# Feed-forward projections: 512-column and 256-column products in runs of eight, or in turn

## The chip, the core and the metric

The kernel runs on one core of a Trainium2 chip. TensorE multiplies matrices and writes to PSUM, VectorE and ScalarE compute on tiles, GpSimd does a few small things, and DMA queues, driven by SyncE, move data from and to device memory. The metric is the device time of one execution, in microseconds, as the median of several runs. All times below are microseconds unless marked ns.

## The reference

A model of two layers on 256 tokens of width 1024, in float32. Each layer is a feed-forward block, a mixer (a gated delta rule with a state-space branch in the first layer, sparse attention in the second) and another feed-forward block; each is followed by a layer norm over the block's output and the scaled input. The change lies in the feed-forward blocks, four of them in all:

```python
D_MODEL, SEQ, D_FF = 1024, 256, 2816

def swiglu(x, w_in, w_out):
    gate, up = jnp.split(x @ w_in, 2, axis=-1)
    return (jax.nn.silu(gate) * up) @ w_out

for layer in range(DEPTH):
    h = layer_norm(DEEPNORM_ALPHA * h + 0.5 * swiglu(h, ffn_w_in[layer, 0], ffn_w_out[layer, 0]), ...)
    ...
    h = layer_norm(DEEPNORM_ALPHA * h + 0.5 * swiglu(h, ffn_w_in[layer, 1], ffn_w_out[layer, 1]), ...)
```

## The kernel before

**Numbers in two parts.** TensorE reads its operands in a reduced float32 format. To keep the accuracy, each operand is split into a high part (the value rounded to that format) and a low part (the rest). A product is then high times high, plus low times high, plus high times low. For weights, `split` does this: a copy to `whi` (ScalarE, or VectorE where the planner finds that better) and a subtraction into `wlo` (always VectorE). The activations `x` are kept as one tile that holds, for each of 8 blocks of 128 input channels, the 256 tokens' high parts and next to them their 256 low parts.

**The feed-forward block** (`ffn`). For each block of 128 of the 2816 hidden channels, `proj_two` computes the gate and then, in a second call, the up projection: 8 blocks of input channels are summed into one PSUM bank `ps` of 512 columns. The weights stand still in the array and the activations move through it. With the high weights `w[0]`, all 512 columns of `x[2]` go through (high and low activations: two of the three products at once). With the low weights `w[1]`, only the 256 high columns go through, and add to the bank's first 256 columns. A projection is thus 8 matmuls of 512 columns and 8 of 256. Then `add_two` adds the two halves of the bank (a copy by ScalarE, an addition by VectorE), ScalarE applies silu to the gate, VectorE multiplies, and the result `g` is split. Between two such pairs of projections the output products of an earlier block run (`out_mm`, four accumulators `acc`, 12 matmuls of 512 columns). The first one or two steps of a block (256 hidden channels each) take another path, token by token (`proj_tok`), and are not touched. That leaves 20 hidden blocks in the first feed-forward block and 18 in each of the other three.

**What sets the order.** All stages record their operations in a plan; `Plan.order` then simulates the engines with a table of costs, picks at each moment the operation that can start first (by priority where several can), hands out buffers, and may choose between engines where an operation has an alternative. The program is written out in that order, and each engine runs its own list in order. In TensorE's list the matmuls of one projection mostly stand in the order in which `proj_two` records them; here and there the planner puts a transpose between them. Buffers: 4 raw weight tiles of 2048 columns, 36 tiles of 1024 columns for everything else, of which the split weights may hold 12 to 24; 2 banks `ps`, 2 `mp` and 4 `acc`.

**Names in the profile.** All instructions carry line 529, where the plan is written out, so tiles tell them apart. `ps<-x,whi` with 512 columns and `ps<-x,wlo` with 256 columns are the two kinds of matmul of `proj_two`, and `acc<-whi,g` and `acc<-wlo,g` the output products; `PEld` are the loads of weights into the array.

Of the kernel before, what the change touches and what calls it, by code (L numbers as in the profile page):

```python
# [21 lines left out]
KD = D // P  # L22
# [530 lines left out]
class K:  # L553
# [174 lines left out]
    def proj_two(self, x, w):  # L728


        ps = self.bank("ps")
        mm = self.nc.tensor.matmul
        for k in range(KD):
            mm(ps, w[0][:, k, :], x[2][:, k].rearrange("p h b t -> p (h b t)"), start=k == 0, stop=False)
        for k in range(KD):
            mm(ps[:, :T], w[1][:, k, :], self.xk(x, k)[0], start=False, stop=k == KD - 1)
        return ps

# [1267 lines left out]
```

## Time and profile before

| | |
|---|---|
| time, median of 3 runs | 1116.87 (1116.46 to 1117.02) |
| the profiled execution's own time | 1116.44 |
| its span, first to last instruction | 1114.7 |
| matmuls | 6528 |
| matmuls of 512 columns in `proj_two` | 1184 |
| VectorE busy | 878.9 (79%) |
| ScalarE busy | 532.2 (48%) |

A row of the timeline reads: start, time from the first start to the last end, engine, line, operation, tile written and tiles read, shape of the standing operand, shape of the result, count. Neighbours of one kind are merged into one row. Matmuls are pipelined: the next one starts before the one before it has ended, so a row's length says less than the distance of two starts. A row of the chain of waits reads: start, length, engine and tile, count. A row of the groups by shape ends with: busy time, mean ns of one, idle time before them.

### The profile page before, as it was taken

To read this page: it belongs to the slowest core of one execution; us is meant where nothing else is said; L and a number is where in the kernel's file an instruction comes from. 1 tells how busy PE (TensorE), PEld (TensorE's weight loads), DVE (VectorE), ACT (ScalarE), POOL (GpSimd) and SP (SyncE) were. 2 spreads that over 40 slices of the span, in tenths; PEclk is the share of its full clock that TensorE was granted. 3 is DMA by queue.
4 is the path that set the end of the run, shared out by engine and by line. 5 is a ranking of instruction groups with operands and counts; after the bars stand their busy time and mean duration, and the time that the engine had idled before them with its cause. 6 is when DMAs were issued, how large, how long until landed. Compare 5 with 4: busy or idle time off the path is not lost.

```text
span 1114.7 us, 16484 instructions
## 1 busy us (share of the span) xinstructions
PE 1103.0 (99%) x6528; PEld 941.0 (84%) x6528; DVE 878.9 (79%) x1484; ACT 532.2 (48%) x972; POOL 33.8 (3%) x67
## 2 busy tenths in 40 slices
PE   9999999999999999999999999999999999999997
PEld 7888888899999788888888888888878778888886
DVE  8967767878979989777767967876888899677755
ACT  6644333478638656433333633433444766433320
POOL 1000000001000210000000000000000000000000
PEclk9999999999999999999999999999999999999999
DMA  9966563642633385755563755555445128655511
GB/s 332 347 197 213 186 225 113 227 139 76 221 121 133 120 275 186 249 203 177 189 223 115 259 196 193 189 188 160 151 157 184 45 93 281 224 189 201 177 39 38
DMA packets 151672, 201.56 MB, mean 181 GB/s; under 512 B 9565, under 2 KB 127786, under 8 KB 151594
## 3 DMA queue, kind: packets, MB, share of 16 engines
q1 hardware_dynamic: 151594, 200.50, 53.9%
q8 instruction: 51, 0.84, 0.3%
q14 instruction: 27, 0.22, 0.1%
HBM read 197.18 MB, written 1.07 MB: 178 GB/s over the span
## 4 chain that ended last, share of the span: by engine, by line
PE 93%; DVE 4%; DMA 1%; ACT 1%; issue 0%; POOL 0%; SPq 0%; DVEq 0%; POOLq 0%
PE ps L529 57%; PE acc L529 31%; PE mp L529 5%; DVE arena L529 1%; DVE wlo L529 1%; DMA G<-cum 1%; ACT P L529 1%; DVE cv L529 0%; DMA raw<-in_ffn_w_in_dram 0%; ACT G L529 0%; DVE o L529 0%; DVE qs L529 0%; DVE y L529 0%; POOL arena L529 0%; DVE G L529 0%
## 5 line engine op out<-in xcount | busy, mean ns | idle before, releaser
L529 DVE TENSOR_TENSOR wlo<-raw,whi 128x1024 fp32r<-128x1024 f32 (+1 forms) x348 | 415.0, 1214 | 9.5 <-ACT whi L529 6.6
L529 PE MATMUL ps<-x,whi 128*128 128x512 f32 (+1 forms) x1600 | 375.3, 365 | 0.6 <-ACT ktok L529 0.4
L529 PEld LDWEIGHTS ps<-x,whi 128*128 128x128 f32 x1600 | 282.8, 189 | 46.9 <-issue 2.1
L529 ACT ACTIVATE whi<-raw 128x1024 fp32r<-128x1024 f32 (+1 forms) x260 | 262.0, 1050 | 11.5 <-DMA raw<-in_ffn_w_in_dram 9.9
L529 PE MATMUL acc<-whi,g 128*128 128x512 f32 x704 | 230.6, 391 | 0.0
L529 ACT ACTIVATE sg<-ps 128x256 f32<-128x256 f32 x162 | 62.2, 384 | 350.0 <-PE ps L529 349.9
L529 PE MATMUL ps<-x,wlo 128*128 128x256 f32 x1392 | 224.9, 283 | 0.0
L529 PEld LDWEIGHTS ps<-x,wlo 128*128 128x128 f32 x1392 | 201.2, 190 | 11.6
L529 DVE TENSOR_TENSOR sg<-ps,sg 128x256 f32<-128x256 f32 x162 | 68.7, 424 | 161.1 <-ACT sg L529 160.8
L529 PEld LDWEIGHTS acc<-whi,g 128*128 128x128 f32 x704 | 132.5, 188 | 25.9
L529 PE MATMUL acc<-wlo,g 128*128 128x512 f32 x352 | 138.1, 392 | 0.0
L529 PE MATMUL ps<-whi,x 128*128 128x512 f32 (+1 forms) x480 | 129.4, 385 | 0.5 <-DVE whi L529 0.2
L529 PEld LDWEIGHTS ps<-whi,x 128*128 128x128 f32 x480 | 85.9, 189 | 17.7 <-issue 1.6
L529 PEld LDWEIGHTS acc<-wlo,g 128*128 128x128 f32 x352 | 66.4, 189 | 10.9
L529 PE MATMUL ps<-wlo,x 128*128 128x512 f32 (+1 forms) x240 | 67.9, 381 | 0.5 <-DVE wlo L529 0.5
L529 PE MATMUL acc<-whi,x 128*128 128x512 f32 x192 | 64.1, 403 | 0.1
L529 DVE CAST whi<-raw 128x1024 fp32r<-128x1024 f32 (+2 forms) x88 | 59.7, 680 | 1.8 <-PE acc L529 1.3
L529 PEld LDWEIGHTS ps<-wlo,x 128*128 128x128 f32 x240 | 43.2, 188 | 8.1 <-DVE wlo L529 1.2
L529 ACT ACTIVATE sg<-sg 128x256 f32<-128x256 f32 x74 | 31.0, 419 | 33.9 <-DVE sg L529 33.8
L529 DVE SCALAR_TENSOR_TENSOR cv<-cv,arena 128x255 f32<-128x255 f32 (+2 forms) x84 | 39.7, 477 | 5.7 <-ACT cv L529 5.1
L529 PEld LDWEIGHTS acc<-whi,x 128*128 128x128 f32 x192 | 35.6, 188 | 7.5 <-issue 0.5
L529 PE MATMUL acc<-wlo,x 128*128 128x512 f32 x96 | 37.7, 396 | 0.0
(247 smaller groups left out, 950.0 us busy)
## 6 DMA issues: line engine op xcount, KB each, us to landing
raw<-in_ffn_w_in_dram SPq DMA_DIRECT2D x74, 1024.0 KB, 5.1
raw<-in_ffn_w_out_dram SPq DMA_DIRECT2D x44, 1024.0 KB, 5.0
raw<-in_hyb_w_in_dram SPq DMA_DIRECT2D x20, 1024.0 KB, 5.1
raw<-in_ffn_w_in_dram SPq DMA_DIRECT2D x24, 512.0 KB, 5.0
raw<-in_hyb_w_out_dram SPq DMA_DIRECT2D x8, 1024.0 KB, 4.9
raw<-in_nsa_w_in_dram SPq DMA_DIRECT2D x5, 1024.0 KB, 5.2
raw<-in_nsa_w_out_dram SPq DMA_DIRECT2D x4, 1024.0 KB, 5.0
w<-in_nsa_cmp_w_dram SPq DMA_DIRECT2D x8, 512.0 KB, 9.0
```

What stands on the lines that cost most here:

```text
L529: r = getattr(getattr(nc, eng), fn)(*[res(a) for a in args], **{k: res(a) for k, a in kw.items()})
```

## The change

One loop over the 8 blocks of input channels takes the place of two. For each block it issues the matmul with high weights and then the one with low weights; before, eight with high weights came first and then eight with low weights. The sums are the same, added in another order.

```diff
         mm = self.nc.tensor.matmul
         for k in range(KD):
             mm(ps, w[0][:, k, :], x[2][:, k].rearrange("p h b t -> p (h b t)"), start=k == 0, stop=False)
-        for k in range(KD):
             mm(ps[:, :T], w[1][:, k, :], self.xk(x, k)[0], start=False, stop=k == KD - 1)
         return ps
```

TensorE's list at the first two projections of the program, in the first feed-forward block, before (`ps_288` and `ps_328` are the gate's and the up projection's banks, `mp` takes transposes, `acc_359` is the first accumulator of the output products):

```order
L529 MATMUL mp_283<-ident_130,sg_242 128x128 x2
L529 MATMUL ps_288<-x_164,whi_246 128x512 x5
L529 MATMUL mp_302<-ident_130,sg_286 128x128 x2
L529 MATMUL ps_288<-x_164,whi_246 128x512 x3
L529 MATMUL ps_288<-x_164,wlo_255 128x256 x8
L529 MATMUL ps_328<-x_164,whi_267 128x512 x8
L529 MATMUL ps_328<-x_164,wlo_280 128x256 x8
L529 MATMUL acc_359<-whi_297,g_291 128x512
```

The same place after the change, around the second pair of transposes:

```order
L529 MATMUL ps_288<-x_164,wlo_255 128x256
L529 MATMUL ps_288<-x_164,whi_246 128x512
L529 MATMUL mp_304<-ident_130,sg_286 128x128 x2
L529 MATMUL ps_288<-x_164,wlo_255 128x256
L529 MATMUL ps_288<-x_164,whi_246 128x512
```

Three matmuls of 512 columns and three of 256 stand ahead of the second row (the first row is the last of them), in turn, so the low weights `wlo_255` are read from the projection's second matmul on, where they were read from its ninth on. The pair of transposes that stood behind five matmuls of 512 columns now stands behind four of 512 and three of 256.

At the end of the second projection, where the rows before (above) go from eight matmuls on `wlo_280` to `acc_359`, TensorE's list now reads:

```order
L529 MATMUL ps_328<-x_164,wlo_280 128x256
L529 MATMUL ps_328<-x_164,whi_267 128x512
L529 MATMUL ps_328<-x_164,wlo_280 128x256
L529 MATMUL acc_359<-whi_298,g_291 128x512
L529 MATMUL acc_359<-wlo_325,g_291 128x512
```

One matmul of 256 columns stands before the output products, where eight stood. Away from the projections the planner's lists hardly differ: four pairs of transposes stand at another place inside a projection, two copies to `whi` move from ScalarE to VectorE, and in the last block a few operations of ScalarE and VectorE change places by one. The DMAs are the same, in the same order.

## The prediction

> **What bounds the kernel now.** I read the page first (busy time, granted clock, shares of the chain), then the groups by shape, then the chain in order of time, and last the timeline of TensorE in single stretches.
>
> ```profile
> span 1114.7 us, 16484 instructions
> PE 1103.0 (99%) x6528; PEld 941.0 (84%) x6528; DVE 878.9 (79%) x1484; ACT 532.2 (48%) x972; POOL 33.8 (3%) x67
> PEclk9999999999999999999999999999999999999999
> PE 93%; DVE 4%; DMA 1%; ACT 1%; issue 0%; POOL 0%; SPq 0%; DVEq 0%; POOLq 0%
> ```
>
> TensorE is busy for 99% of the span, its clock is granted in full in every slice, and 93% of the chain that ended last is its own. A busy row can overlap its neighbours, so what counts is not the length of a row but the step from the start of one matmul to the start of the next. That step is the whole question here, because the change alters nothing but the order of matmuls.
>
> ```profile
> L529 PE MATMUL ps<-x,whi 128*128 128x512 f32 x1184 | 294.8, 391 | 0.0
> L529 PE MATMUL ps<-x,wlo 128*128 128x256 f32 x1392 | 224.9, 283 | 0.0
> ```
>
> A **long** matmul has 512 columns (high weights), a **short** one 256 (low weights). The 1184 long ones belong to proj_two alone: 8 each, so 148 projections, which the feed-forward blocks make in 74 pairs (gate and up). As many shorts go with them (the other 208 are another stage's).
>
> **The steps now.** The chain in order of time shows one pair of projections as a piece of 32 matmuls on ps, and the output products between pairs as a piece on acc.
>
> ```profile
> 37.65 5.56 PE ps L529 x32
> ...
> 162.25 5.56 PE ps L529 x32
> ...
> 569.49 2.75 PE acc L529 x12
> ...
> 599.99 8.87 PE acc L529 x39
> ```
>
> Both acc pieces are longs that follow a run of shorts. 39 less 12 is 27 more longs in 8.87 - 2.75 = 6.12 us: a settled long steps by **0.2267 us**. Twelve of those make 2.720, and the piece takes 2.75: some 0.03 us is lost once at its head, after the shorts. From 37.65 to 162.25 lie 15 whole periods, 8.307 us each, of 16 + 12 = 28 longs and 16 shorts.
>
> ```profile
> 563.76 1.98 PE L529 MATMUL ps<-x,whi 128*128 128x512 f32 x8
> 565.58 1.11 PE L529 MATMUL ps<-x,wlo 128*128 128x256 f32 x8
> 566.53 2.00 PE L529 MATMUL ps<-x,whi 128*128 128x512 f32 x8
> 568.37 1.12 PE L529 MATMUL ps<-x,wlo 128*128 128x256 f32 x8
> 569.32 0.40 PE L529 MATMUL acc<-whi,g 128*128 128x512 f32 x1
> ```
>
> Here is one pair. The longs of the gate, which follow longs, take 565.58 - 563.76 = 1.82 us; those of the up projection, which follow shorts, take 1.84; eight shorts take 0.95, so 0.119 each, and I use **0.120**. With 0.2267 and 0.120 the period would be 28 x 0.2267 + 16 x 0.120 = 8.267; it is 8.307. The 0.040 left over is the **recovery**: after each of the two short runs of a period the next few longs are together about 0.020 us late. Runs of eight pay for it twice in a period.
>
> **What the change does to the steps.** It adds no instruction and takes none away; 16 shorts and 16 longs of a pair still run, now one by one in turn. The traces hold no stretch of regular alternation, so its step has to be bounded. The nearest rows are in the attention stage, where single short mask products stand among longs.
>
> ```profile
> 858.16 0.28 PE L529 MATMUL ps<-fixed 128*128 128x256 f32 x1
> 858.27 0.40 PE L529 MATMUL ps<-whi,x 128*128 128x512 f32 x1
> 858.50 0.40 PE L529 MATMUL ps<-wlo,x 128*128 128x512 f32 x1
> 858.74 0.39 PE L529 MATMUL ps<-whi,x 128*128 128x512 f32 x1
> 858.97 0.63 PE L529 MATMUL acc<-kd,qs 128*128 128x512 f32 x2
> 859.43 0.28 PE L529 MATMUL acc<-fixed 128*128 128x256 f32 x1
> ...
> 861.84 0.28 PE L529 MATMUL ps<-fixed 128*128 128x256 f32 x1
> 861.95 0.28 PE L529 MATMUL acc<-fixed 128*128 128x256 f32 x1
> 862.07 0.63 PE L529 MATMUL ps<-kd,qs 128*128 128x512 f32 x2
> 862.54 0.28 PE L529 MATMUL ps<-fixed 128*128 128x256 f32 x1
> 862.65 0.62 PE L529 MATMUL acc<-kd,qs 128*128 128x512 f32 x2
> 863.11 0.28 PE L529 MATMUL acc<-fixed 128*128 128x256 f32 x1
> ```
>
> First stretch: one short, then five longs, 859.43 - 858.16 = 1.27 us. The short itself steps by 0.11, less than 0.120, but the five longs after it take 859.43 - 858.27 = 1.16, that is 0.232 each. So a lone short with room to recover costs 1.27 - 5 x 0.2267 = 0.137: one short starts as full a recovery as a run of eight does. Second stretch, the densest mixture in the trace: three shorts and four longs, with no room to recover between, in 863.11 - 861.84 = 1.27 us, and 1.27 - 4 x 0.2267 = 0.363, so 0.121 for each short. There the recovery is cut off before it costs much.
>
> Regular alternation has one long between shorts, nearer to the second stretch than to the first. I take **0.120 + 0.2267 = 0.3467 us** for a short and a long together, and one recovery where the pair ends and the longs of acc begin.
>
> **The sum.** Before, a period has 0.040 of recovery; after, 0.020. That is 0.020 x 74 pairs = 1.5 us less. The profiled execution took 1116.44 us (1114.7 of span and 1.7 around it); 1116.44 - 1.5 = 1114.9. The three runs have their median 0.43 above the profiled execution, at 1116.87, so I predict 1116.87 - 1.5 = **1115.4 us**. For the unknown step both ends are kept: a pair of matmuls may take 0.340 (short at half a settled long, long settled) or 0.363 (0.2267 and the lone short's 0.137).
>
> **What else moves, at nothing.** A projection ends with the same short matmul as before, so ScalarE and VectorE get its bank at the same time. The low weights are needed earlier: after one long instead of eight, so 7 x 0.2267 = 1.6 us sooner. That could be a new wait, above all at the start of the program, where weights have just landed. In the order they are written in, the first projection's low weights are VectorE's row at 16.69, the second's the one at 19.89:
>
> ```profile
> 16.69 1.22 DVE L529 TENSOR_TENSOR wlo<-raw,whi 128x1024 fp32r<-128x1024 f32 x1
> ...
> 19.89 1.22 DVE L529 TENSOR_TENSOR wlo<-raw,whi 128x1024 fp32r<-128x1024 f32 x1
> ```
>
> ```profile
> 20.52 1.41 PE L529 MATMUL ps<-x,whi 128*128 128x512 f32 x5
> ...
> 23.64 2.00 PE L529 MATMUL ps<-x,whi 128*128 128x512 f32 x8
> ```
>
> They are ready at 17.91 and 21.11. In the changed order the first short of these projections is due one long after their start, at 20.75 and 23.87: 2.8 us of room in either. Later ones have more, since the writes run further and further ahead:
>
> ```profile
> L529 DVE TENSOR_TENSOR wlo<-raw,whi x348: 735/1219/1228, 8.0 to 1072.9; 128x1024 fp32r<-128x1024 f32 x171, 128x840 fp32r<-128x840 f32 x2, 128x560 fp32r<-128x560 f32 x1
> L529 PE MATMUL acc<-wlo,g x352: 389/389/481, 26.7 to 1106.6; 128*128 128x512 f32 x176
> ```
>
> The last low weights begin to be written at 1072.9, and the last product that reads such weights starts at 1106.6, over 30 us later. The high weights' buffers come free later, since the last long now stands next to last: by the seven shorts that stood behind it, 7 x 0.120 = 0.8 us. The writer that waits for a buffer is that far ahead of TensorE, and this room hides 0.8; without it each of the 148 projections could lose up to 0.8. Where two transposes stand inside a projection they stay after about as much matmul time: five longs before, 5 x 0.2267 = 1.13, against four longs and three shorts now, 1.27, so what they wait for is no later than they. Two high-weight copies go from ScalarE to VectorE, both off the path (48% and 79% busy). I count all of this as nothing.
>
> **The rivals.**
>
> Rival 1, **the shorts get faster**. A short that follows a long steps by 0.11 in both stretches above, not by 0.120; only the following shorts of a run are at 0.120. In alternation every short follows a long. If the weight load is what holds a run of shorts at 0.120, a long before each short takes that away, and if the longs stay settled the pair is 0.2267 + 0.1133 = 0.340. Sixteen make 5.440, with 2.75 of acc 8.190 against 8.307: 0.117 x 74 = 8.6 us less, 1108.2. For it: the last two longs of the second stretch take 863.11 - 862.65 = 0.46, 0.23 each. Against it: where the short took 0.11 in the first stretch, the next two longs took 0.23 and 0.24, so the gain was given back at once.
>
> ```profile
> L529 PEld LDWEIGHTS ps<-x,wlo 128*128 128x128 f32 x1392 | 201.2, 190 | 11.6
> ```
>
> A load's row lasts 190 ns, more than a short's step, so loads overlap matmuls and the row can't say whether it is the limit. The Trainium skill (TensorE: Matmul & The Clock Gate, LDWEIGHTS (loading the stationary operand)) gives a load as its number of columns over 1.2 ns, an estimate of 107 ns for 128 columns. By that rule the load fits under a step of 0.113, nothing would hold a short at 0.120 once the load starts in time, and this rival's time would come true; the 0.119 of a run of shorts in this trace is longer than the rule gives.
>
> Rival 2, **the recovery never ends**. In runs the longs settle after a few steps and stay at 0.2267 until the next shorts; in alternation each long comes right after a short and none may ever settle. Then every long costs the 0.232 of the first stretch, and the short after an unsettled long has no lead and steps by 0.120: 0.352 for both. Sixteen make 5.632, with 2.75 8.382: 0.075 x 74 = 5.6 us more, 1122.4. This one ends on the other side; it decides from (8.307 - 2.75) / 16 = 0.3473 for both on, where the period gets longer than before. For it: the first two longs after every short run are late. Against: the second stretch.
>
> Rival 3, **a full recovery for each short**, 0.363 for both: 16 x 0.363 + 2.75 = 8.558, 18.6 us more, 1135.5. The second stretch speaks against it, since three shorts there would have cost 0.05 more than they did.
>
> That the change doesn't do what it says can be left out: the order of TensorE's matmuls shows the alternation in all 148 projections.
>
> **How the numbers follow.** My forecast (0.345 to 0.349 for both) has 0.40, rival 1 in full or in part 0.30, rival 2 in full or in part 0.24, rival 3 0.04, and 0.02 are left for a wait on weights or buffers. A change of 0.2%, 2.2 us, is about what a measurement can tell from none; 2.2 / 74 = 0.030 in a period, so it begins at 0.3454 for both below and at 0.3492 above. The forecast's band touches the lower edge, so faster is 0.36, same 0.36, slower 0.28. Cases of both signs hold most of the chance: the forecast's own range is 1113 to 1118. The range for 8 in 10 takes in rivals 1 and 2 in full, 1108.0 to 1123.0, and leaves out rival 3.
>
> **What the changed profile will show.** The chain's piece on ps of 32 matmuls, now 5.56 us, decides: 5.55 by the forecast, 5.44 by rival 1, 5.63 by rival 2, 5.81 by rival 3. The piece on acc should stay at 2.75. TensorE should wait for no low weights near 20 us. I would be wrong if the step of a long depended on something that only alternation has, such as the two column counts writing the same bank in turn, which no row of this trace shows.

## The result, and the profile after

The changed kernel takes 1122.2 us in the median of five runs, against 1116.84 before (five runs): ratio 1.0053, interval 1.0039 to 1.0067. It is slower by 5.4 us, where 1.5 us less was forecast; the time lies within the stated range, near rival 2's 1122.4.

The page after (span and instructions, busy time of the engines, granted clock, shares of the chain that ended last):

```profile
span 1119.8 us, 16483 instructions
PE 1108.6 (99%) x6528; PEld 939.6 (84%) x6528; DVE 880.2 (79%) x1486; ACT 529.8 (47%) x970; POOL 33.8 (3%) x67
PEclk9999999999999999999999999999999999999999
PE 93%; DVE 4%; ACT 1%; DMA 1%; issue 0%; POOL 0%; SPq 0%; DVEq 0%; POOLq 0%
```

The limit is the same: as many matmuls, TensorE 99% busy, clock granted, 93% of the chain. The span is 5.1 us longer, and TensorE's busy time 5.6. TensorE's list of waits holds none above 1.1 us in either kernel, and those that differ are of 0.5 us or less. The time did not go into a wait but into the matmuls' own steps. The chain in order of time shows where:

```profile
457.04 8.17 PE acc L529 x36
...
565.85 5.64 PE ps L529 x32
571.49 2.75 PE acc L529 x12
574.23 5.64 PE ps L529 x32
...
602.32 8.87 PE acc L529 x39
```

The piece of 32 matmuls, a pair of projections, went from 5.56 to 5.64 us; the piece on acc stayed at 2.75. 0.08 x 74 pairs = 5.9 us, a little more than the measured 5.1 of span. One feed-forward block, from the acc piece at its one end to that at the other, shows the same. Its rows in the chain of the kernel before:

```profile
456.06 8.19 PE acc L529 x36
...
599.99 8.87 PE acc L529 x39
```

That is 143.93 us from one start to the other, against 602.32 - 457.04 = 145.28 after: 1.35 more for the block's 18 pairs, 0.075 each.

Inside the piece the timeline after reads (start, length, tiles, shape):

```profile
565.68 0.39 PE L529 MATMUL ps<-x,whi 128*128 128x512 f32 x1
565.91 0.28 PE L529 MATMUL ps<-x,wlo 128*128 128x256 f32 x1
566.02 0.40 PE L529 MATMUL ps<-x,whi 128*128 128x512 f32 x1
566.26 0.28 PE L529 MATMUL ps<-x,wlo 128*128 128x256 f32 x1
566.38 0.40 PE L529 MATMUL ps<-x,whi 128*128 128x512 f32 x1
566.62 0.28 PE L529 MATMUL ps<-x,wlo 128*128 128x256 f32 x1
566.74 0.40 PE L529 MATMUL ps<-x,whi 128*128 128x512 f32 x1
566.97 0.28 PE L529 MATMUL ps<-x,wlo 128*128 128x256 f32 x1
...
569.09 0.28 PE L529 MATMUL ps<-x,wlo 128*128 128x256 f32 x1
```

The first long, which follows the output products, steps by 0.23, and the first short by 0.11. From then on every long is late: 566.02 to 566.26, 566.38 to 566.62, 566.74 to 566.97, 0.23 to 0.24 each against a settled 0.2267. From 565.91 to 569.09 stand nine shorts and nine longs in 3.18 us, **0.3533 us for a short and a long together** where 0.3467 was forecast.

To the nanosecond the trace's starts show a rhythm that repeats every three pairs of matmuls. The table gives, for each step inside a pair of projections and the first matmuls on acc behind it, how much longer it is in ns than a settled long (L, 226.7) or a short within a run (S, 120); it is the mean over the 70 of 74 pairs that no transpose interrupts, rounded; they agree to a nanosecond.

```
before  L0 x8 | S-7 S-1 S0 x6 | L+7 L+9 L+2 L+6 L+4 L0 L0 L0 | S-7 S-1 S0 x6 | L+7 L+9 L+2 L+6 L+4 L0 ...
after   L0 | S-7 L+6 S-3 L+14 S0 L+9 | S-7 L+6 S-3 L+14 S0 L+9 | ... | S-7 | L+6 L+9 L+2 L+6 L+4 L0 ...
```

Before, the sum of a run of shorts and the recovery behind it is -8 + 28 = 20 ns, twice in a period, as the prediction has it. After, the three pairs of a rhythm add up to -7 + 6 - 3 + 14 + 9 = 19 ns (20 unrounded), over and over: every three shorts cost what a run of eight cost before. Five such rhythms and the recovery behind the last short make 120 ns in a period, where two recoveries made 40. In the changed kernel the longs never settle, until the output products give them room.

The low weights came in time. VectorE's first rows, then TensorE's first shorts of the first two projections:

```profile
16.43 1.22 DVE L529 TENSOR_TENSOR wlo<-raw,whi 128x1024 fp32r<-128x1024 f32 x1
...
19.64 1.22 DVE L529 TENSOR_TENSOR wlo<-raw,whi 128x1024 fp32r<-128x1024 f32 x1
```

```profile
20.60 0.28 PE L529 MATMUL ps<-x,wlo 128*128 128x256 f32 x1
...
23.63 0.28 PE L529 MATMUL ps<-x,wlo 128*128 128x256 f32 x1
```

Ready at 17.65 and 20.86, used at 20.60 and 23.63: 2.8 us of room or more, as predicted.

### The profile page after: what moved, and what is told of

Read it like the earlier page. It is cut to its first block, busy times and chain, and to the rows that moved or that the text cites. A ratio compares the mean times of both kernels' runs of the same rounds, so it can differ in the third digit from the quotient of the medians.

```text
span 1119.8 us, 16483 instructions
## 1 busy us (share of the span) xinstructions
PE 1108.6 (99%) x6528; PEld 939.6 (84%) x6528; DVE 880.2 (79%) x1486; ACT 529.8 (47%) x970; POOL 33.8 (3%) x67
## 4 chain that ended last, share of the span: by engine, by line
PE 93%; DVE 4%; ACT 1%; DMA 1%; issue 0%; POOL 0%; SPq 0%; DVEq 0%; POOLq 0%
PE ps L529 57%; PE acc L529 31%; PE mp L529 5%; DVE arena L529 1%; DVE wlo L529 1%; DMA G<-cum 1%; ACT P L529 1%; DVE cv L529 0%; DMA raw<-in_ffn_w_in_dram 0%; ACT G L529 0%; DVE o L529 0%; DVE qs L529 0%; DVE y L529 0%; POOL arena L529 0%; DVE G L529 0%
## 5 line engine op out<-in xcount | busy, mean ns | idle before, releaser
L529 PE MATMUL ps<-x,whi 128*128 128x512 f32 (+1 forms) x1600 | 501.6, 370 | 0.5 <-ACT ktok L529 0.4
L529 PE MATMUL ps<-x,wlo 128*128 128x256 f32 x1392 | 391.8, 282 | 0.0
L529 PEld LDWEIGHTS ps<-x,whi 128*128 128x128 f32 x1600 | 287.7, 189 | 59.0 <-issue 2.1
L529 ACT ACTIVATE whi<-raw 128x1024 fp32r<-128x1024 f32 x258 | 259.8, 1050 | 12.8 <-DMA raw<-in_ffn_w_in_dram 11.2
L529 PEld LDWEIGHTS ps<-x,wlo 128*128 128x128 f32 x1392 | 263.2, 189 | 2.9
```

The source lines that it names most:

```text
L529: r = getattr(getattr(nc, eng), fn)(*[res(a) for a in args], **{k: res(a) for k, a in kw.items()})
```

## The experiments

All differ from the kernel before or from the change in `proj_two` alone, or in one function that makes both projections of a pair. Ratios are to the kernel before in the same comparison. The period is the distance of two starts in the chain (a pair of projections and 12 output products); it was 8.307 before and is 8.387 after. In every experiment it answers for the time: its difference from 8.307, times 74, is within 1.4 us of what the time moved.

### Runs of another length

**One run of sixteen shorts.** Gate and up projection are made by one function, which issues eight longs of the gate, one long of the up projection, all sixteen shorts and then seven longs. In the code, `long(ps, w, k)` and `short(ps, w, k)` issue one matmul for block `k` into bank `ps`.

```diff
-                self.add_two(sg, self.proj_two(x, wg[e]))
+                pg, pu = self.proj_pair(x, wg[e], wu[e])
+                self.add_two(sg, pg)
                 nc.scalar.activation(sg, sg, AF.Silu)
-                self.add_two(up, self.proj_two(x, wu[e]))
+                self.add_two(up, pu)
...
+        for k in range(KD):
+            long(pg, wg, k)
+        long(pu, wu, 0)
+        for k in range(KD):
+            short(pg, wg, k)
+        for k in range(KD):
+            short(pu, wu, k)
+        for k in range(1, KD):
+            long(pu, wu, k)
```

> Gate and up projection are computed together: eight longs of the gate, one of the up projection, then all sixteen shorts in one run, then the other seven longs. Theory S (each change from shorts to longs costs; about 0.020 us where the longs have room to settle, about half a hundredth where they have not): one recovery in a period in place of two, so the piece of 32 matmuls takes 5.56 to 5.57, the piece on acc right behind longs only 2.72 to 2.74, and the time is 0.020 x 74 = 1.5 us below the kernel before: 1115.4, ratio 0.9987. Theory N (the cost goes with the number of shorts, not of changes): the same as before, ratio 1.000.

Measured: 1114.67, ratio 0.9986 (0.9977 to 0.9994). The chain:

```profile
546.63 5.57 PE ps L529 x32
552.20 2.72 PE acc L529 x12
554.92 5.57 PE ps L529 x32
```

Theory S holds: one recovery in a period of 8.287, and the output products behind settled longs take 2.72. The planner here also gives 65 operations of VectorE to ScalarE; the kernel of fourteen and two shorts, below, has the same steps up to its two shorts without that.

**Runs of four, runs of two.** `R` stands for 4 or 2; the edit is shown against the kernel before.

```diff
-        for k in range(KD):
-            mm(ps, w[0][:, k, :], x[2][:, k].rearrange("p h b t -> p (h b t)"), start=k == 0, stop=False)
-        for k in range(KD):
-            mm(ps[:, :T], w[1][:, k, :], self.xk(x, k)[0], start=False, stop=k == KD - 1)
+        for k0 in range(0, KD, R):
+            for k in range(k0, k0 + R):
+                mm(ps, w[0][:, k, :], x[2][:, k].rearrange("p h b t -> p (h b t)"), start=k == 0, stop=False)
+            for k in range(k0, k0 + R):
+                mm(ps[:, :T], w[1][:, k, :], self.xk(x, k)[0], start=False, stop=k == KD - 1)
```

> Runs of four longs and four shorts in a projection. Theory S: four changes from shorts to longs in a period, each with three to four longs to settle in, so 0.015 to 0.020 each, 0.06 to 0.08 in a period against 0.040 before: 1.5 to 3 us slower than the kernel before, 1118.3 to 1119.8. Theory N: as before, 1116.8.

> Runs of two. Theory S: eight changes in a period, cut off after two longs (0.233 and 0.236 us, 0.016 late together, less what the first short gains): 0.07 to 0.13 in a period against 0.040: 2 to 7 us slower than the kernel before, 1119 to 1124. Theory N: as before, 1116.8.

Measured: runs of four 1119.62, ratio 1.0028 (1.0018 to 1.0038); runs of two 1115.1, ratio 0.9989 (0.9979 to 0.9999). Four is slower, as theory S has it, but by more: 3.6 us than the kernel before in the same comparison (1116.06), where 1.5 to 3 were expected, and 0.087 is lost in a period, where 0.06 to 0.08 were expected. The output products behind its last run take 2.77:

```profile
548.28 5.58 PE ps L529 x32
553.87 2.77 PE acc L529 x12
```

Two is not as theory S has it: it is no slower but a little faster than before, with eight changes from shorts to longs in a period. The chain of runs of two, a pair of projections and the output products behind it:

```profile
545.89 5.56 PE ps L529 x32
551.45 2.73 PE acc L529 x12
554.18 5.56 PE ps L529 x32
```

So the cost is not a price for each change. The steps say why:

```
runs of two    L0 L0 | S-7 S-1 L+7 L+9 S-4 S-8 L+6 L+4 | S-7 S-1 L+7 L+9 S-4 S-8 L+6 L+4 | ...
runs of four   L0 x4 | S-7 S-1 S0 S0 L+7 L+9 L+2 L+6 S-3 S-1 S-3 S-3 L+8 L+7 L+9 L-2 | S-3 S0 S0 S0 L+7 ...
```

In runs of two, the shorts that come after two late longs are early by 4 and 8, and the two longs after them, late by 6 and 4, are the last late ones: the second time the sum is almost nothing, and the steps are settled again. Two runs of two cost 7 ns together (6 by the rounded steps), in place of 20 for one run of eight.

**A run of fourteen, then one of two.** That gives a prediction: after any run of shorts, two longs, two shorts and two longs should end the recovery early. The edit is shown against one run of sixteen.

```diff
-        for k in range(KD):
+        for k in range(KD - 2):
             short(pu, wu, k)
-        for k in range(1, KD):
+        for k in (1, 2):
+            long(pu, wu, k)
+        for k in (KD - 2, KD - 1):
+            short(pu, wu, k)
+        for k in range(3, KD):
             long(pu, wu, k)
```

> As with one run of sixteen shorts, but only fourteen stand in the run; two longs, then the last two shorts, then the other five longs follow. Theory P (how late a matmul starts depends only on the column counts of the last few, as runs of two showed: two longs late by 7 and 9 ns, two shorts early by 4 and 8, two longs late by 7 and 4, then settled): the pattern costs about 0.007 us in a period where the single run costs 0.020, so the period is 8.273 to 8.275 and the time 2.5 us below the kernel before, ratio 0.9978. Theory S (every change from shorts to longs costs about 0.020 where room follows): two changes, at least as slow as one run of sixteen, ratio 0.9986 or above.

Measured: 1114.26, ratio 0.9979 (0.997 to 0.9988), the fastest of the kernels that compute every product. The chain and one pair's timeline:

```profile
546.60 5.55 PE ps L529 x32
552.15 2.72 PE acc L529 x12
554.87 5.55 PE ps L529 x32
```

```profile
565.02 1.84 PE L529 MATMUL ps<-x,wlo 128*128 128x256 f32 x14
566.70 0.63 PE L529 MATMUL ps<-x,whi 128*128 128x512 f32 x2
567.17 0.39 PE L529 MATMUL ps<-x,wlo 128*128 128x256 f32 x2
567.39 1.31 PE L529 MATMUL ps<-x,whi 128*128 128x512 f32 x5
```

The period is 8.273, the steps behind the fourteen shorts L+7 L+9 S-4 S-7 L+6 L+4 L0: theory P's sequence, and not S. How late a matmul starts follows from the column counts of the matmuls ahead of it, and can be read off one sequence and used in another. That the last few are enough, as theory P says, is not so: inside the alternation every long has the same neighbours for many matmuls back, and is late by 6, 14 and 9 in turn. The place in the rhythm, counted from the last settled stretch, matters too.

### What it is not: the bank, the columns, the room for a load

**The shorts add to the other half of the bank**, and **neighbours write different banks** (a short of the gate stands between longs of the up projection, then the other way round):

```diff
-            mm(ps[:, :T], w[1][:, k, :], self.xk(x, k)[0], start=False, stop=k == KD - 1)
+            mm(ps[:, T:], w[1][:, k, :], self.xk(x, k)[0], start=False, stop=k == KD - 1)
```

```diff
+        long(pg, wg, 0)
+        long(pu, wu, 0)
+        for k in range(1, KD):
+            short(pg, wg, k - 1)
+            long(pu, wu, k)
+        short(pg, wg, KD - 1)
+        for k in range(1, KD):
+            long(pg, wg, k)
+            short(pu, wu, k - 1)
+        short(pu, wu, KD - 1)
```

> Alternation as in the change, but the shorts add to the second 256 columns of the bank in place of the first; the sum of the two halves is the same. Theory B (a short and the long next to it add to the same 256 columns of one bank too soon after each other): the distance between two additions to a column is another, so the steps change, and the time goes below 1121 or above 1124. Theory S: the same steps, 113, 233, 117, 241, 120, 236 ns in turn, piece of 32 matmuls 5.64, time 1122.2.

> Both banks are open at once; a short of one projection alternates with a long of the other, so neighbours write different banks. Theory B (collision in one bank): the excess goes, 16 pairs of matmuls take 5.55 to 5.57. Theories S, L and W: the same steps as in the change, 0.353 for a short and a long together; the whole time within 1 us of 1122.2 unless both banks' eviction at the end of the pair makes TensorE wait.

Measured: 1122.29, ratio 1.0051 (1.0037 to 1.0065), and 1121.64, ratio 1.0047 (1.0032 to 1.0062). In both the rhythm of three pairs is there, S-7 L+6 S-3 L+14 S0 L+9. The second, whose order differs at the ends of a pair (it opens with two longs and closes with two shorts), has a period of 8.373, the first 8.387 as the change. Where the products are added plays no part in the rhythm: theory B falls.

**Shorts of 384 columns**, alternating and in runs of eight:

```diff
-            mm(ps[:, :T], w[1][:, k, :], self.xk(x, k)[0], start=False, stop=k == KD - 1)
+            mm(ps[:, :384], w[1][:, k, :], x[2][:, k].rearrange("p h b t -> p (h b t)")[:, :384], start=False, stop=k == KD - 1)
```

> Alternation with shorts of 384 columns in place of 256 (the low weights also multiply the first 128 tokens' low parts: extra work). By a settled long's rate such a short steps by 0.173 us, with a long 0.400, sixteen 6.40. Theory L (a weight load is too slow to be done under a short of 0.120 us; the long behind it starts late): a load fits under 0.173 with room, so no excess at all: piece of 32 matmuls 6.39 to 6.40, the same as runs of eight of 384. Theory W (any change of the column count unsettles the steps, whatever room the loads have): excess as in the change, 0.10 more, 6.49 to 6.50, and 5 us slower than runs of 384.

> Runs of eight longs and eight shorts as before, shorts of 384 columns (extra work as in the alternating twin). Theory L: no recovery is left, the period is 28 x 0.2267 + 16 x 0.1733 = 9.12 and the time 1116.8 + 74 x (9.12 - 8.307) = 1177. Theory W: two recoveries of 0.020 in a period as before, 9.16, 1180, and longs behind shorts again step by 0.233 and 0.236.

Measured: 1184.6, ratio 1.0614 (1.0598 to 1.063), alternating; 1186.48, ratio 1.0629 (1.0613 to 1.0645), in runs. The alternating kernel's timeline:

```profile
549.23 0.33 PE L529 MATMUL ps<-x,wlo 128*128 128x384 f32 x1
549.40 0.39 PE L529 MATMUL ps<-x,whi 128*128 128x512 f32 x1
...
550.85 0.34 PE L529 MATMUL ps<-x,wlo 128*128 128x384 f32 x1
```

Four shorts and four longs in 1.62 us, 0.405 for both, and over the whole piece 6.50 where 6.40 would be settled: 0.10 of excess, 0.006 for each of the 16 short-long pairs, about as much as with 256 columns (5.64 - 16 x 0.3467 = 0.09). The 0.173 in this sum is not a settled long's rate, as the expectation has it; that would be 0.2267 x 384 / 512 = 0.170. It lies half-way from 0.120 to 0.2267, and the last two shorts of a run of 384 do step by 0.1733. Theory L, as stated, falls, for a short of 0.17 us leaves a load more room than one of 0.12, and the excess is there. But theory W missed too: with 384 columns runs of eight lose as much inside the piece (6.49) and more behind it, since those shorts are late themselves (by 2, 4, 12, 3 and 8 ns over 173.3, from the second to the sixth of the first run). Here alternation is the faster of the two.

### Narrower loads

**High weights of 64 columns from the second block on** (alternating as in the change), **low weights of 64 columns up to the last block**, **both**, and **runs of eight with narrow high weights**. The kernels leave out half of the products with the weights that they narrow. The first uses the first three lines of the edit alone, the second the last three, the third all, and the fourth the first three in the kernel before:

```diff
+            m = P if k == 0 else 64
-            mm(ps, w[0][:, k, :], x[2][:, k].rearrange("p h b t -> p (h b t)"), start=k == 0, stop=False)
+            mm(ps[:m], w[0][:, k, :m], x[2][:, k].rearrange("p h b t -> p (h b t)"), start=k == 0, stop=False)
...
+            m = P if k == KD - 1 else 64
-            mm(ps[:, :T], w[1][:, k, :], self.xk(x, k)[0], start=False, stop=k == KD - 1)
+            mm(ps[:m, :T], w[1][:, k, :m], self.xk(x, k)[0], start=False, stop=k == KD - 1)
```

> Alternation as in the change; from the second block of input channels on the high weights are only 64 of the 128 hidden channels (half of the high products are left out), so the load that runs under a short is half as wide. Theory L: it now fits under the short; no excess, piece of 32 matmuls at most 5.55, and the time at most 1115.5. Theory W: the step sequence stays, 5.64 and 1122.2.

> Alternation as in the change; the low weights are only 64 of the 128 hidden channels wide, but in the last block (half of the low products are left out), so the load under a long is narrow and the load under a short is full. Each full load delays the matmul it runs under by 13 ns and a half one by 7, which gives 0.340 for a pair of matmuls without excess. Theory Q (the excess of the alternation comes from the full load under a short): it stays, about 0.0067 for a pair, piece of 32 matmuls 5.53 to 5.55. Theory R (any narrower load gives enough room): no excess, 5.44 to 5.46.

> Alternation with both weights 64 wide except in the first block of the high and the last of the low (half of the products are left out). A load of half width costs the matmul it runs under 7 ns: a short steps by 0.113, a long by 0.220, together 0.333, piece of 32 matmuls 5.34 to 5.37 with the few full loads. If instead the 13 ns of a step are a fixed cost of a matmul, not of its load: 0.347 and 5.55.

> Runs of eight as before, with the high weights 64 wide from the second block on (half of the high products left out). Loads of half width run under the longs and under the last short of the gate's run. Theory Q: longs 0.220, the up projection's longs behind the shorts settled at once but for its first, full, load; piece of 32 matmuls 5.46 to 5.48, the piece on acc behind it 2.75 with its recovery, as its loads are full. Theory R: the recovery inside the piece also goes, and nothing else differs. If the recovery belongs to the change of column count alone, the up projection's longs are late by 7 and 9 ns as before: 5.48 to 5.50.

| narrow | median | ratio | interval | piece of 32 | period |
|---|---|---|---|---|---|
| high, alternating | 1109.6 | 0.9944 | 0.9928 to 0.9961 | 5.45 | 8.200 |
| low, alternating | 1118.88 | 1.002 | 1.001 to 1.003 | 5.56 | 8.340 |
| both, alternating | 1111.05 | 0.9957 | 0.9942 to 0.9972 | 5.48 | 8.227 |
| high, runs of eight | 1118.22 | 1.0016 | 1.0006 to 1.0026 | 5.58 | 8.327 |

With narrow high weights the alternation reaches what rival 1 hoped for; theory L's forecast holds here, and theory W's falls. The timeline (128*64 is the standing operand):

```profile
560.21 0.39 PE L529 MATMUL ps<-x,whi 128*64 128x512 f32 x1
560.44 0.28 PE L529 MATMUL ps<-x,wlo 128*128 128x256 f32 x1
...
562.25 0.39 PE L529 MATMUL ps<-x,whi 128*64 128x512 f32 x1
```

Six longs and six shorts in 2.04 us, 0.340 for both: longs settled, shorts at half of a long, S-7 L0 again and again. Only behind the up projection's first high weights, which are 128 wide, are two longs late, by 6 and 3. Its groups by shape show what was halved:

```profile
L529 PEld LDWEIGHTS ps<-x,whi 128*64 128x64 f32 x1036 | 138.9, 134 | 40.5
L529 PEld LDWEIGHTS ps<-x,whi 128*128 128x128 f32 x564 | 93.1, 190 | 10.7 <-issue 2.1 <-ACT cv L529 1.6 <-ACT ktok L529 0.6
```

134 ns in place of 190, 56 ns less for 64 columns. So the width of the high weights does decide whether alternation is smooth. It can't be separated here from the number of rows that the matmul writes, which it also sets.

The loads' rows also say whether theory L can be saved by taking the row's length, and not a shorter time, for a load. In these traces a load begins 1 to 6 ns after the start of the matmul ahead of the one that it serves. One load for a long behind a short, with shorts of 384 columns and then with narrow high weights:

```profile
549.23 0.19 PEld L529 LDWEIGHTS ps<-x,whi 128*128 128x128 f32 x1
```

```profile
560.10 0.13 PEld L529 LDWEIGHTS ps<-x,whi 128*64 128x64 f32 x1
```

The longs that they serve start at 549.40 and 560.21, before the rows have ended: by the trace's nanoseconds 15 to 21 ns before in the first kernel, and 24 in the second. By the row, then, the load fits under the short in neither, yet the longs of the first take longer steps and those of the second settled ones. Whether the row fits does not decide it either.

Narrow low weights help less: 5.56 for the piece, 0.01 above theory Q's range, with an irregular rhythm that Q did not foresee, and theory R falls. Their load runs under a long, where the full one, of 188 ns, has ended 35 to 50 ns before the next matmul in the changed kernel already; so what they gain is not room for a load.

The sums of the last three expectations set a price that these kernels put to the test, 13 ns for a full load on the matmul above it and 7 for a half one. No earlier run shows this price, and it falls: both narrow gives 5.48, neither 5.34 to 5.37 nor 5.55, and no long ever steps by 0.220. That theory Q's sum came near the measured piece is therefore no support for it. In runs of eight, narrow high weights make the longs themselves irregular (L+9 L+3 L-3 L0 L+8 L+3 L+9 in the first run) and the piece slower, 5.58, where every theory had it faster.

## Why the prediction was wrong

- **What bounds the kernel**: right. TensorE's steps set the time, before and after, and no wait of more than 0.5 us came or went.
- **The recovery** of 0.020 behind each run of shorts: right, confirmed by one run of sixteen in place of two of eight, which gained 1.4 us, where one recovery in each period makes 1.5.
- **The step that failed** is the choice of 0.3467 for a short and a long together, with one recovery behind them. Measured were 0.3533, and 5.64 for the piece where 5.55 was forecast. I took the densest mixture of the attention stage for a stand-in of alternation, as its shorts cost 0.121. But its order is two shorts, two longs, one short, two longs: it has two longs between shorts. Runs of two show that such an order is cheap (8.293 for a period), and strict alternation dear (8.387). The rows were read rightly; what they stood for was not. The first stretch, with one short, had already shown both longs behind a short late, and the alternating kernel just never gets past them.
- **Rival 2** is what happened, with a chance of 0.24: the longs never settle. Its 5.632 for the piece was measured at 5.640. Its parts were off and cancelled: the shorts do step early in two cases of three, 0.117 in the mean and not 0.120, and the longs are late by 10 ns in the mean, 0.2364 and not 0.232. So the closeness of its 1122.4 is in part luck.
- **Rival 1** had the right kind of reason, that a load's length matters, but no kernel with full loads reached its 0.340. The Trainium skill (TensorE: Matmul & The Clock Gate, LDWEIGHTS (loading the stationary operand)) gives a load as columns over 1.2 ns, an estimate of 53 ns for 64 columns; the 56 ns between the two load rows above agree with that, though each row lasts some 80 ns longer than its estimate. What I made of the rule does not hold: an estimated 107 ns fit under a short of 384 columns (0.173) with room, and the excess was there all the same. So that a load fits by this estimate does not make the alternation smooth.
- **Low weights needed earlier, buffers free later, two copies on VectorE**: nothing, as predicted; 2.8 us of room were left.
- **The sums** do not agree among themselves. The prediction's own pieces, 16 x 0.3467 + 2.75 = 8.297, make 0.7 us less, and not 1.5: the 2.75 holds 0.03 of lateness, and 0.020 is what is left of it only where the first shorts of a run are early. And 0.345 to 0.349 for both gives 1114.1 to 1118.9, not 1113 to 1118. Neither changes the outcome.
- **The chances**: 0.36 for faster came from a settled step that no row showed in a steady alternation. With one long between shorts, the row nearest in kind was the first long after a short, always late.

What stays open is the mechanism inside TensorE. The runs show that the steps follow from the column counts and the widths of the standing operands, back to the last settled stretch, and that neither the bank, nor the columns written, nor room for the load alone accounts for them. They do not show which part of the engine the late longs wait for.

## What to carry to other kernels

Where TensorE bounds a kernel, measure the step from start to start, not the busy time, and measure it in the very order that is planned: a mixture that looks alike can have another rhythm. Where two widths are mixed, try fewer changes between them first: here one run of shorts in place of two gained 0.14%, and two of the shorts set two longs behind the rest another 0.07% by the medians (the two intervals overlap; the period is 0.01 us shorter). But count no fixed price for each change: at 256 columns runs of two beat runs of four and of eight, strict alternation was the worst of six orders, and at 384 it was the better of two.

## What the runs showed of the hardware that was not expected

- A matmul's step depends on its neighbours in an exactly repeated way: in 70 pairs of projections, before and after, the steps agree to a nanosecond, and sequences seen in one kernel forecast another (8.273 to 8.275 expected, 8.273 measured).
- A settled matmul with a new standing operand takes 0.2267 us for 512 columns, and half of it, 0.1133, for 256, but the latter right after a settled long, and in strict alternation every third time; in a run of shorts it is 0.120.
- Runs of two cost less than runs of four or eight: 8.293, 8.353 and 8.307 for a period.
- A standing operand of 64 in place of 128 columns for the long matmuls made strict alternation 0.0133 us faster for each short and long together (0.3533 and 0.340).
- In the projections a weight load begins 1 to 6 ns after the start of the matmul ahead of the one that it serves, and its row lasts 186 to 193 ns for 128 columns. In a run of shorts the matmul starts some 75 ns before the row of its load has ended.
